# u and z token-major by seven products, with weight sums added onto kept pages

## The chip, the cores and the metric

The kernel runs on one core of a Trainium2 chip. The metric is the device time of one execution in microseconds; the kernel before has a median of 1637.15 us over three runs (1636.79 to 2001.78).

## The reference

Two layers over 512 tokens of width 2048, in float32. Both begin with a wide projection and end with an output projection, a residual sum and a layer norm. The part that matters here is the odd layer:

```python
def odd_layer(x, w_in, ln_g, ln_b, sgu_w, sgu_b, w_out):
    h = x @ w_in
    uv = jax.nn.gelu(h[..., :2 * D_SGU])
    z = h[..., 2 * D_SGU:]
    u, v = jnp.split(uv, 2, axis=-1)
    v = layer_norm(v, ln_g, ln_b).reshape(bsz, s // SGU_CHUNK, SGU_CHUNK, SGU_GROUPS, SGU_GROUP_DIM)
    w_causal = sgu_w * jnp.tril(jnp.ones((SGU_CHUNK, SGU_CHUNK), sgu_w.dtype))
    mixed = jnp.einsum('gts,bnsgc->bntgc', w_causal, v) + sgu_b.T[:, :, None]
    y = u * mixed.reshape(bsz, s, D_SGU) * jax.nn.silu(z)
    return y @ w_out
```

The even layer mixes a gated short convolution with an attention of three branches over eight heads; its output projection is `wo0`, the odd layer's projections are `wv1` (v), `wuz` (u and z) and `wo1`.

## The kernel before

Every float32 product is made of three products of rounded parts: `split` (lines 84 to 86) casts a page to a high part on ACT and subtracts it on DVE for the low part; then come high x high, high x low, low x high. Weights arrive as pages of 128x1024 (512 KB) from DRAM, asked for by SyncE into `raw` (four buffers); the parts `whi` and `wlo` have four buffers each.

The projections of the even layer go by `unit_a` (line 103): 128 weight columns stand still, 512 tokens move, 48 matmuls to a unit. Then come eight heads (the loop from line 436).

`wo0`, `wv1` and `wo1` go by `strassen` (line 528): the matrix is cut in two along the tokens, the contraction and the columns, and seven products p, in the order 1, 2, 5, 3, 6, 7, 4, take the place of eight. Each is 96 matmuls (lines 591 to 593), with pieces of x, `shi` and `slo`, standing still and a weight page moving. c is the half of a product's contraction, g the column group, m the token tile. Products 5, 7, 6 and 4 need sums of weight blocks. `weight_sums` (line 198) makes them ahead of time in DRAM with POOL's DMAs: a 1x1 copy that orders the step (208), a plain copy (210), an accumulating copy (212), all of 1024 KB blocks. The steps of `wo0` and `wv1` are issued two to a head, those of `wo1` in every second pass of the u/z loop.

u and z (line 817) go feature-major: for each of 16 column tiles j, one unit for u, one for z, then the mixing over positions as four 128x128 float32 matmuls (830) and DVE operations (832 to 835), with `row_sums` (797) once. v is normalised by one operation for each token tile (774). `residual_rows` (803) makes the scaled residual with rows `gb` and stores part of it for the last projection.

`drain` runs deferred work from the list `later`, so many pieces after each column group. The engines' instruction order comes from a scheduler, and POOL, SyncE, ACT and DVE each run theirs in order.

Around the start, `bias_rows` (178) takes two raw pages and line 317 a third, ahead of the next units.

Of the kernel before, what the change touches and what calls it, by code (L numbers as in the profile page):

```python
# [16 lines left out]
P = 128  # L17
# [48 lines left out]
def trunk(ctx, tc, xT, xn, oneh, cst, table, wa, wv, convw, posT, cw1, cw2, wo0, wuz, wv1, odg, odb, sguw, sgub, wo1, out):  # L66
# [102 lines left out]
    lnT = const.tile([P, 2 * KT], F32, name="lnT")  # L169
    convT = const.tile([P, 8, 3], F32, name="convT")  # L170
# [23 lines left out]
    def blk(w, k, n, g, c):  # L194

        return w[4 * (2 * g + n) + 2 * k + c]

    def weight_sums(w, name):

        t = {}  # L200

        def step(q, gcs):
            def run(after=None):

                for g, c in gcs:
                    t[q, g, c] = dram.tile([P, 2048], F32, name=f"{name}{q}{g}{c}")
                    if after is not None:
                        nc.gpsimd.dma_start(t[q, g, c][0:1, 0:1], after)
                    first = {5: lambda: blk(w, 0, 0, g, c), 7: lambda: blk(w, 1, 1, g, c), 6: lambda: t[7, g, c], 4: lambda: t[6, g, c]}[q]()
                    nc.gpsimd.dma_start(t[q, g, c], first)  # L210
# [3 lines left out]
        gcs = [(g, c) for c in range(2) for g in range(2)]  # L214
        return t, [step(q, gcs[i:i + 2]) for q in (5, 7, 6, 4) for i in (0, 2)]

    sums0, steps0 = weight_sums(wo0, "ts0_")
    sumsv, stepsv = weight_sums(wv1, "tsv_")
    sums1, steps1 = weight_sums(wo1, "ts1_")


    with ExitStack() as es:
# [218 lines left out]
        for h in range(NH):  # L441
# [23 lines left out]
            for st in (steps0 + stepsv)[2 * h:2 * h + 2]:  # L465
                st(qT[0:1, 0:1])
# [56 lines left out]
    def rows(ap):  # L523

        return ap if len(ap.shape) == 4 else ap.rearrange("p k (n c) -> p k n c", n=2)

    def strassen(sp, w, sums, a, done, given=None, more=2, by_tile=False, wx=None):
# [9 lines left out]
        def tt(out, x, y, op):  # L537
            nc.vector.tensor_tensor(rows(out), rows(x), rows(y), op)

        def s_piece(p, c, early):  # L540
            if p == 5 and c == 0:
                for d in range(2):
                    tt(a(1, 0, d), a(1, 0, d), a(1, 1, d), ALU.subtract)
            if p == 3 and c == 0:
                for d in range(2):
                    tt(a(0, 0, d), a(1, 0, d), a(0, 0, d), ALU.subtract)
                    tt(a(0, 1, d), a(0, 1, d), a(0, 0, d), ALU.add)
            if p == 6 and c == 0:
                for d in range(2):
                    o, x, y = a(1, 0, d), a(0, 0, d), a(1, 1, d)  # L550
                    for n in range(2) if len(o.shape) == 4 else (slice(None),):
                        nc.vector.scalar_tensor_tensor(o[:, :, n], x[:, :, n], -1.0, y[:, :, n], ALU.mult, ALU.subtract)
            if given and p in (1, 2, 4):
                return given(p, c)
            src = {1: a(0, 0, c), 2: a(0, 1, c), 5: a(1, 0, c), 3: a(0, 1, c), 7: a(1, 0, c), 6: a(0, 0, c), 4: a(1, 1, c)}[p]
            if early:
                hi = wp.tile([P, 4, 256], F32R, tag="hi", name="shi", bufs=4)
                lo = wp.tile([P, 4, 256], F32R, tag="lo", name="slo", bufs=4)
            else:
                hi = sp.tile([P, 4, 256], F32R, tag="shi", name="shi", bufs=2)  # L560
                lo = sp.tile([P, 4, 256], F32R, tag="slo", name="slo", bufs=2)
            split(rows(hi), rows(lo), rows(src))
            return hi, lo

        def unit(p, g, c):
            src = sums[p, g, c] if p in (5, 7, 6, 4) else blk(w, *{1: (0, 0), 2: (1, 0), 3: (1, 1)}[p], g, c)
            parts = []
            for d in range(2):
                raw = raw_page()
                nc.sync.dma_start(raw, src[:, d * 1024:(d + 1) * 1024])  # L570
                pool = wx if wx and count[0] % 2 else wp
                count[0] += 1
                hi = pool.tile([P, 1024], F32R, tag="hi", name="whi", bufs=4)
                lo = pool.tile([P, 1024], F32R, tag="lo", name="wlo", bufs=4)
                split(hi, lo, raw)
                parts.append((hi, lo))
            return parts

        banks = {}

        def product(p, g, c, m, s, parts):
            new = p in (1, 5, 7, 6)
            if new and c == 0:
                banks[g, m, p] = bank()
            b = banks[g, m, {2: 1, 3: 5, 4: 7}.get(p, p)]
            ms = slice(m * P, m * P + P)
# [105 lines left out]
    def normalized(m):  # L692
# [10 lines left out]
        def turn(c):  # L703
# [12 lines left out]
            split(act_hi[:, 4 * c:4 * c + 4, m * P:(m + 1) * P], act_lo[:, 4 * c:4 * c + 4, m * P:(m + 1) * P], dst)  # L716
# [12 lines left out]
    strassen(sp, wo0, sums0, quarters(y_sb), prefill)  # L729
# [35 lines left out]
    def given(p, c):  # L765
        t, k = {1: (0, 0), 2: (0, 1), 4: (1, 1)}[p]
        k0 = 8 * k + 4 * c
        return act_hi[:, k0:k0 + 4, t * 256:(t + 1) * 256], act_lo[:, k0:k0 + 4, t * 256:(t + 1) * 256]

    strassen(sp, wv1, sumsv, xq, done_v, given)  # L770
    drain(len(later))
    for m in range(NT):
        mv, rs = moments(statsv, m, EPS)
        nc.vector.tensor_scalar(xv[:, m], xv[:, m], mv[:, 0:1], rs, ALU.subtract, ALU.mult)
    sp_.close()


    yv = xv.rearrange("p n (j c) -> p j n c", c=P)
    xr = big.tile([P, NT, DM], F32, tag="big0", name="xr")
    with tc.tile_pool(name="sgu", bufs=2) as sg:  # L780
        swT = sg.tile([P, 8, P], F32, name="swT", bufs=1)
        nc.sync.dma_start(swT, sguw)
        tril = sg.tile([P, P], F32, name="tril", bufs=1)
        nc.sync.dma_start(tril, cst[:, P + NT:P + NT + P])
        nc.vector.tensor_tensor(swT, swT, tril[:, None, :].to_broadcast([P, 8, P]), ALU.mult)
        ones = sg.tile([P, P], F32, name="ones", bufs=1)
        nc.vector.memset(ones, 1.0)
        sbb = sg.tile([P, 8, P], F32, name="sbb", bufs=1)
        nc.sync.dma_start(sbb, sgub.to_broadcast([P, 8 * P]).rearrange("p (g t) -> p g t", g=8))
        ogT = sg.tile([P, 2, KT], F32, name="ogT", bufs=1)  # L790
        nc.sync.dma_start(ogT, odb)
        rw = sg.tile([P, 8, P], F32, name="rw", bufs=1)

        def row_sums():
            for c in range(2):
                ps = bank()
                nc.tensor.matmul(ps, ones, swT[:, 4 * c:4 * c + 4, :], start=True, stop=True)
                nc.vector.tensor_copy(rw[:, 4 * c:4 * c + 4, :], ps.rearrange("p (g t) -> p g t", g=4))

        def chunks(t):  # L800
            return t.rearrange("p (n t) -> p n t", n=NT)

        def residual_rows(g):

            cs = slice(g * 512, (g + 1) * 512)
            gb = sg.tile([P, 2, 512], F32, name="gb", bufs=1)
            for i in range(2):
# [159 lines left out]
```

## Time and profile before

| what | us |
|---|---|
| median of three runs | 1637.15 |
| the profiled execution | 1635.04 |
| its span, first to last instruction | 1633.0 |
| TensorE busy | 1603.1 |
| DVE busy | 859.1 |
| ACT busy | 589.6 |

The span holds the even layer with its heads (to about 772 us), `wo0` (to about 930), `wv1` (to 1110), u and z (to 1456), `wo1` (to about 1618) and the last rows. The profiled execution's time is 2.0 us longer than its span. Matmuls overlap in the records: the mean time of one is longer than the distance from one to the next.

### The profile page before, as it was taken

What the parts mean: (1) busy time and instruction counts of PE and PEld (TensorE: products, weight loads), DVE (VectorE), ACT (ScalarE), POOL (GpSimd) and SP (SyncE); (2) the same over time, 40 slices, a digit from 0 to 9 for tenths busy, and PEclk for the clock granted to TensorE, in tenths of its full rate; (3) what the DMA queues carried; (4) which work ended last, traced back from release to release, by engine and by line L of the source; (5) the groups of instructions that cost most, each with busy time, mean ns of one, the idle gap of its engine ahead of it and who ended that gap; (6) DMA issues with size and microseconds to landing.
All of it is one profiled execution on the core that took longest, in us unless ns stands there. A gap on an engine that the chain in (4) does not pass through costs nothing.

```text
span 1633.0 us, 19377 instructions
## 1 busy us (share of the span) xinstructions
PE 1603.1 (98%) x7527; PEld 1335.9 (82%) x7527; DVE 859.1 (53%) x1323; ACT 589.6 (36%) x859; POOL 150.7 (9%) x236
## 2 busy tenths in 40 slices
PE   8999999999999999999999999999999999998996
PEld 6798888888898888888888788888888888886884
DVE  5234444535325454445668985876433333355788
ACT  4123232323223232332555875542222222234641
POOL 0101020101001101010010000000111111100101
PEclk9999999999999999999999999999999999999998
DMA  6549595959249495866786665685777765669953
GB/s 218 196 152 271 135 250 132 267 158 247 76 154 243 149 243 156 217 184 179 217 243 205 239 217 193 199 306 181 220 198 200 195 189 167 182 181 293 274 190 135
DMA packets 98008, 328.56 MB, mean 201 GB/s; under 512 B 11443, under 2 KB 12243, under 8 KB 96380
## 3 DMA queue, kind: packets, MB, share of 16 engines
q1 hardware_dynamic: 65228, 217.30, 39.6%
q0 software_dynamic: 32544, 109.61, 28.8%
q8 instruction: 59, 0.97, 0.2%
q10 hardware_dynamic: 144, 0.41, 0.1%
q14 instruction: 33, 0.27, 0.1%
HBM read 315.72 MB, written 114.84 MB: 264 GB/s over the span
## 4 chain that ended last, share of the span: by engine, by line
PE 93%; issue 2%; DVE 2%; DMA 2%; ACT 0%; POOL 0%; SPq 0%; POOLq 0%; DVEq 0%
PE ps L111 19%; PE ps L113 19%; PE ps L112 19%; PE ps L593 8%; PE ps L592 8%; PE ps L591 8%; PE ps_t L397 1%; PE ps L122 1%; PE ps L120 1%; PE ps L121 1%; PE hp L286 1%; PE pm L830 1%; PE po L340 1%; PE po L342 1%; PE po L341 1%
## 5 line engine op out<-in xcount | busy, mean ns | idle before, releaser
L86 DVE TENSOR_TENSOR wlo<-raw,whi 128x1024 fp32r<-128x1024 f32 (+2 forms) x358 | 429.8, 1205 | 587.1 <-ACT whi L85 577.1
L85 ACT CAST whi<-raw 128x1024 fp32r<-128x1024 f32 (+2 forms) x358 | 371.1, 1038 | 908.8 <-PE ps L112 568.7
L111 PE MATMUL ps<-act_hi,whi 128*128 128x512 f32 x1376 | 542.4, 394 | 0.0
L113 PE MATMUL ps<-act_hi,wlo 128*128 128x512 f32 x1376 | 537.4, 391 | 1.3 <-DVE wlo L86 1.3
L112 PE MATMUL ps<-act_lo,whi 128*128 128x512 f32 x1376 | 535.4, 389 | 0.0
L113 PEld LDWEIGHTS ps<-act_hi,wlo 128*128 128x128 f32 x1376 | 258.3, 188 | 58.2 <-DVE wlo L86 1.7
L112 PEld LDWEIGHTS ps<-act_lo,whi 128*128 128x128 f32 x1376 | 258.5, 188 | 53.2
L111 PEld LDWEIGHTS ps<-act_hi,whi 128*128 128x128 f32 x1376 | 258.6, 188 | 51.1
L591 PE MATMUL ps<-whi,shi 128*128 128x512 f32 x576 | 224.6, 393 | 4.3 <-ACT ua L643 4.3
L593 PE MATMUL ps<-whi,slo 128*128 128x512 f32 x576 | 225.4, 392 | 0.6 <-DVE slo L86 0.5
L592 PE MATMUL ps<-wlo,shi 128*128 128x512 f32 x576 | 225.0, 391 | 0.2 <-DVE wlo L86 0.2
L591 PEld LDWEIGHTS ps<-whi,shi 128*128 128x128 f32 x576 | 108.1, 188 | 28.5 <-ACT ua L643 5.2
L593 PEld LDWEIGHTS ps<-whi,slo 128*128 128x128 f32 x576 | 108.2, 188 | 25.2 <-DVE slo L86 1.9
L592 PEld LDWEIGHTS ps<-wlo,shi 128*128 128x128 f32 x576 | 108.2, 188 | 24.9 <-DVE wlo L86 1.6
L212 POOL DMA_DIRECT2D ts<-in_wo_dram x32 | 33.2, 1038 | 161.5 <-DMA ts<-in_wo_dram 82.5
L378 ACT ACTIVATE t_sc<-t_sc,mx 128x128 f32<-128x128 f32 (+1 forms) x64 | 35.1, 550 | 17.2 <-DVE mx L375 17.2
L677 POOL TENSOR_TENSOR rs<-mv,epst 128x1 f32<-128x1 f32 x12 | 14.7, 1232 | 287.9 <-DVE mv L675 287.9
L591 PE MATMUL ps<-whi,act_hi 128*128 128x512 f32 x96 | 38.0, 399 | 0.6 <-ACT whi L85 0.6
L592 PE MATMUL ps<-wlo,act_hi 128*128 128x512 f32 x96 | 38.0, 396 | 0.0
L593 PE MATMUL ps<-whi,act_lo 128*128 128x512 f32 x96 | 37.9, 395 | 0.0
L122 PE MATMUL ps<-whi,act_lo 128*128 128x268 f32 x128 | 36.9, 288 | 0.0
L121 PE MATMUL ps<-wlo,act_hi 128*128 128x268 f32 x128 | 36.8, 288 | 0.0
(204 smaller groups left out, 1358.1 us busy)
## 6 DMA issues: line engine op xcount, KB each, us to landing
raw<-in_wa_dram SPq DMA_DIRECT2D x110, 512.0 KB, 5.3
ts<-in_wo_dram POOLq DMA_DIRECT2D x32, 1024.0 KB, 14.8
raw<-ts SPq DMA_DIRECT2D x64, 512.0 KB, 4.7
raw<-in_wuz_dram SPq DMA_DIRECT2D x64, 512.0 KB, 4.9
raw<-in_wo_dram SPq DMA_DIRECT2D x48, 512.0 KB, 5.2
tsv<-in_wv_dram POOLq DMA_DIRECT2D x16, 1024.0 KB, 12.9
raw<-tsv SPq DMA_DIRECT2D x32, 512.0 KB, 3.9
raw<-in_wv_dram SPq DMA_DIRECT2D x24, 512.0 KB, 3.9
```

The costliest lines, as they stand in the source:

```text
L85: nc.scalar.copy(hi, src)
L86: nc.vector.tensor_tensor(lo, src, hi.bitcast(F32), ALU.subtract)
L111: nc.tensor.matmul(ps, hi[:, w], act_hi[:, kt, :], start=kt == 0, stop=False)
L112: nc.tensor.matmul(ps, hi[:, w], act_lo[:, kt, :], start=False, stop=False)
L113: nc.tensor.matmul(ps, lo[:, w], act_hi[:, kt, :], start=False, stop=kt == KT - 1)
L121: nc.tensor.matmul(ps[:, :width], act_hi[:, kt, ms], lo[:, w], start=False, stop=False)
L122: nc.tensor.matmul(ps[:, :width], act_lo[:, kt, ms], hi[:, w], start=False, stop=kt == KT - 1)
L212: nc.gpsimd.dma_start(t[q, g, c], blk(w, *{5: (0, 1), 7: (0, 1), 6: (0, 0), 4: (1, 0)}[q], g, c), accum_op=ALU.add, max_dma_last_dim=2048)
L378: nc.scalar.activation(t[:, offs[qb]:offs[qb] + nk], t[:, offs[qb]:offs[qb] + nk], AF.Exp, bias=mx[:, qb:qb + 1], accum_out=sm[:, qb:qb + 1])
L591: nc.tensor.matmul(b, s[0][:, k, ms], hi[:, ws], start=new and c == 0 and k == 0, stop=False, **kw)
L592: nc.tensor.matmul(b, s[0][:, k, ms], lo[:, ws], start=False, stop=False, **kw)
L593: nc.tensor.matmul(b, s[1][:, k, ms], hi[:, ws], start=False, stop=c == 1 and k == 3, **kw)
```

## The change

- u and z are made in two runs r of `strassen`, each over half the columns of both. Their weight pages are four pieces of 256 columns (1 KB runs); the moving operand is then four pieces of 128 columns with a stride (`cuts`).
- The mixing is token-major: `swT` standing tiles and 256 columns a matmul; the bias is one number for each partition (`sbT`). v is normalised in pieces of 512 columns with rows (`values`), the residual rows likewise with tiles `xs` (two buffers) and `row` (one buffer).
- y is transposed on TensorE (`y_turn`) and copied by ACT, and goes to `wo1` from there. The rounded copies `act_hi` and `act_lo` of x in the odd layer go, `x_sums` keeps the sums of x apart in `exq`.
- `wuz` gets all four sums for both runs; `wo0`, `wv1`, `wo1` keep only the one for product 7 in DRAM. For 5, 6 and 4, `chained` loads a page x once (eight kept pages) and adds a block onto it by a POOL DMA before each of these products. The steps of sums, 20 of them, each of two blocks in 512 KB halves, are issued two or three to a head; the two steps of `wo1` at the head of u/z.
- Two more raw pages, two small transposes and a small store stand in the setup.
- The wide rows `gb` of the end are loaded after product 6 instead of 5. For the last product of `wo1`, only the second half goes tile by tile. The extra weight buffers there are two instead of four.

```diff
+    def uz_blocks(r):
+        def get(k, n, g, c, d):
+            q, e = 2 * r + g, (2 * k + c) * 512 + d * 256
+            return wuz[8 * q + n:8 * q + 8:2, :, e:e + 256].rearrange("i p e -> p i e")
...
-                    nc.gpsimd.dma_start(t[q, g, c], blk(w, *{5: (0, 1), 7: (0, 1), 6: (0, 0), 4: (1, 0)}[q], g, c), accum_op=ALU.add, max_dma_last_dim=2048)
+                    for d in range(2):
+                        src = get(*more[q], g, c, d)
+                        nc.gpsimd.dma_start(same(t[q, g, c, d], src), src, accum_op=ALU.add, max_dma_last_dim=1024)
...
+    sums0, steps0 = weight_sums(blocks(wo0), (7,), "ts0_")
+    early = steps0 + stepsv + stepsu[0] + stepsu[1]
...
+        bcol = raw_page()[:8, :P]
+        nc.sync.dma_start(bcol, sgub.rearrange("o (g t) -> (o g) t", g=8))
+        nc.tensor.transpose(ps[:, :8], bcol, ident[:8, :8])
+        ocol = raw_page()
+        nc.sync.dma_start(ocol[:, :2 * KT], odb.rearrange("p i k -> p (i k)"))
+        nc.tensor.transpose(ps[:2 * KT, :P], ocol[:, :2 * KT], ident)
...
-            for st in (steps0 + stepsv)[2 * h:2 * h + 2]:
+            for st in early[5 * h // 2:5 * (h + 1) // 2]:
...
+    def chained(get, sums, pool, direct):
+        def unit(p, g, c, d):
+            if p == 1 and c not in direct:
+                return page(g, c, d)
+            if p in (1, 2, 3):
+                if p == 2 and c in direct:
+                    page(g, c, d)
+                return raw_load(get(*{1: (0, 0), 2: (1, 0), 3: (1, 1)}[p], g, c, d))
+            if p == 7:
+                return raw_load(sums[p, g, c, d])
+            nc.gpsimd.dma_start(x[g, c, d], get(*{5: (0, 1), 6: (1, 1), 4: (1, 0)}[p], g, c, d), accum_op=ALU.add)
+            return x[g, c, d]
...
-        for j in range(KT):
-            ps = unit_a(wuz[2 * j])
-            ps = unit_a(wuz[2 * j + 1])
...
+        def one(m):
+            if m == 0:
+                gb[0] = row_pair(odrow, q)
+            v = xv[:, m, q * 512:(q + 1) * 512]
+            nc.vector.scalar_tensor_tensor(v, v, mom[m][0][:, 0:1], gb[0][:, 0], ALU.subtract, ALU.mult)
+            nc.vector.scalar_tensor_tensor(v, v, mom[m][1], gb[0][:, 1], ALU.mult, ALU.add)
...
+        def gate(t, g, m):
+            nc.vector.scalar_tensor_tensor(u[t, g, m], u[t, g, m], YSCALE, z[t, g, m], ALU.mult, ALU.mult)
+            for i in range(2):
+                nc.tensor.matmul(pm[:, i * 256:i * 256 + 256], swT[:, 2 * q + i, :], xv[:, mt, cs], start=True, stop=True)
+            for i in range(2):
+                nc.vector.scalar_tensor_tensor(xv[:, mt, cs], pm[:, i * 256:i * 256 + 256], sbT[:, 2 * q + i:2 * q + i + 1],
+                                               u[t, g, m][:, i * 256:i * 256 + 256], ALU.add, ALU.mult)
+            if r == 1:
+                later.append(lambda: y_turn(mt, q))
...
+        for r in range(2):
+            for q in (2 * r, 2 * r + 1):
+                values(q)
+            for q in (2 * r, 2 * r + 1):
+                residual_rows(q)
+            for st in steps1 if r == 0 else ():
+                st(swT[0:1, 0, 0:1])
+            strassen(sp, x_sums, plain(uz_blocks(r), sumsu[r]), uz_done(r), cuts=True)
...
-        strassen(sp, wo1, sums1, yq, take1, by_tile=True, wx=wx)
+        strassen(sp, in_place(yT), chained(blocks(wo1), sums1, fin, (0, 1)), take1, by_tile=True, wx=wx)
```

In the start, SyncE's loads stood like this before, where `in_odg` is the third raw page and `in_wa` a unit's weight pages:

```order
L184 DMA raw<-in_table_dram 32x8
L317 DMA raw<-in_odg_dram 32x128
L97 DMA raw<-in_wa_dram 128x1024 x2
L284 DMA raw<-in_cw_dram 128x1024 x2
L97 DMA raw<-in_wa_dram 128x1024 x2
```

And like this now, with `in_sgub` for bcol and `in_odb` for ocol:

```order
L186 DMA raw<-in_table_dram 32x8
L339 DMA raw<-in_odg_dram 32x128
L344 DMA raw<-in_sgub_dram 8x128
L349 DMA raw<-in_odb_dram 128x32
L97 DMA raw<-in_wa_dram 128x1024 x2
L306 DMA raw<-in_cw_dram 128x1024 x2
```

Two loads into raw pages moved in ahead of the unit's two weight pages.

At the head of u/z, DVE has in the first run's second half of product 1 and in product 2 (`xv` with `row` is v's normalising, `wlo` and `slo` the low parts of weights and of x):

```order
L86 TENSOR_TENSOR wlo<-raw,whi 128x1024
L873 SCALAR_TENSOR_TENSOR xv<-xv,mv,row 128x512 x2
L874 SCALAR_TENSOR_TENSOR xv<-xv,rs,row 128x512 x2
L86 TENSOR_TENSOR slo<-y_sb,shi 128x1024
L86 TENSOR_TENSOR wlo<-raw,whi 128x1024 x2
L873 SCALAR_TENSOR_TENSOR xv<-xv,mv,row 128x512 x2
L874 SCALAR_TENSOR_TENSOR xv<-xv,rs,row 128x512 x2
L86 TENSOR_TENSOR wlo<-raw,whi 128x1024 x2
```

Where one pass of j had four low parts and five other operations in 22.9 us, here four operations on v stand between each two low parts of the weights.

At the end of u/z TensorE went before from the last mixing straight into `wo1` (lines 591 to 593):

```order
L113 MATMUL ps<-act_hi,wlo 128x512
L830 MATMUL pm<-swT,xv 128x128 x4
L591 MATMUL ps<-whi,shi 128x512
L592 MATMUL ps<-wlo,shi 128x512
L593 MATMUL ps<-whi,slo 128x512
```

And now, where `pm` is the mixing, `ps_y` the transposes of y and lines 655 to 657 the products:

```order
L656 MATMUL ps<-wlo,shi 128x512
L657 MATMUL ps<-whi,slo 128x512
L897 MATMUL ps_y<-ident,xv 128x128 x8
L917 MATMUL pm<-xv,swT 128x256 x4
L897 MATMUL ps_y<-ident,xv 128x128 x6
L655 MATMUL ps<-whi,shi 128x512
L897 MATMUL ps_y<-ident,xv 128x128 x2
L656 MATMUL ps<-wlo,shi 128x512
```

The last two mixings and four groups of transposes stand in TensorE's order around `wo1`'s first matmul.

## Rows read from the trace of the kernel before

**Rows 1.** The page: the span, and each engine's busy time.

```profile
span 1633.0 us, 19377 instructions
...
PE 1603.1 (98%) x7527; PEld 1335.9 (82%) x7527; DVE 859.1 (53%) x1323; ACT 589.6 (36%) x859; POOL 150.7 (9%) x236
```

**Rows 2.** Busy time by stretch: us, five engines, granted clock, DMA share, GB/s.

```profile
880.00:930.00 50.00, 50.00 (x238) 41.38 (x237) 48.85 (x77) 35.81 (x49) 2.44 (x3) 1.00 0.64 221
...
1110.00:1456.00 346.00, 346.00 (x1574) 285.66 (x1573) 135.41 (x164) 79.02 (x92) 29.27 (x42) 1.00 0.66 187
...
1480.00:1500.00 20.00, 15.71 (x68) 12.15 (x66) 10.85 (x9) 9.03 (x11) 0.00 (x0) 1.00 1.07 305
```

**Rows 3.** TensorE's waits: for what, us in total, times, the longest.

```profile
PE ps L591 <- ACT ua L643: 4.3, 2, 2.5
```

**Rows 4.** ACT's timeline before 1491 us: start, length, line, what; idle before it.

```profile
1489.77 1.04 ACT L85 CAST whi<-raw 128x1024 fp32r<-128x1024 f32 x1 [1.75 <-DMA raw<-in_wo_dram]
1490.72 0.58 ACT L643 COPY ua<-ps 128x512 f32<-128x512 f32 x1
```

**Rows 5.** The chain of waits, TensorE's transposes, row sums and mixing: start, length.

```profile
903.33 0.87 PE ps_x L708 x8
...
1110.08 1.72 PE ps L797 x4
...
1157.57 0.89 PE pm L830 x8
...
1180.45 0.89 PE pm L830 x8
```

**Rows 6.** Groups of instructions by form: busy us, mean ns; idle before.

```profile
L86 DVE TENSOR_TENSOR wlo<-raw,whi 128x1024 fp32r<-128x1024 f32 x342 | 416.2, 1222 | 542.2 <-ACT whi L85 532.2 <-PE pm L830 4.3 <-PE ps_t L397 4.2
...
L830 PE MATMUL pm<-swT,xv 128*128 128x128 f32 x128 | 16.9, 275 | 0.0
...
L286 PE MATMUL hp<-tokb,raw 128*128 128x62 f32 x128 | 14.9, 288 | 0.0
...
L833 DVE SCALAR_TENSOR_TENSOR ug<-ug,th 128x512 f32<-128x512 f32 x16 | 11.1, 691 | 0.4
```

**Rows 7.** TensorE's timeline after the bias rows.

```profile
56.15 0.24 PE L319 MATMUL ps<-ident,raw 32*128 32x32 f32 x1
56.32 0.50 PE L111 MATMUL ps<-act_hi,whi 128*128 128x512 f32 x1
```

**Rows 8.** SyncE's timeline there: when the next page is asked for.

```profile
56.25 0.35 SPq L97 DMA_DIRECT2D raw<-in_wa_dram  x1
```

**Rows 9.** DMA issues: count, KB each, median us from issue to landing.

```profile
ts<-in_wo_dram POOLq DMA_DIRECT2D x32, 1024.0 KB, 14.8
...
raw<-in_wuz_dram SPq DMA_DIRECT2D x64, 512.0 KB, 4.9
...
xr<-xhat SPq DMA_DIRECT2D x16, 256.0 KB, 6.1
...
xres<-xr SPq DMA_DIRECT2D x12, 256.0 KB, 2.3
...
gb<-in_odg_dram SPq DMA_DIRECT2D x8, 256.0 KB, 5.2
```

**Rows 10.** The page's DMA queues: packets, MB, share of 16 engines' span.

```profile
q1 hardware_dynamic: 65228, 217.30, 39.6%
q0 software_dynamic: 32544, 109.61, 28.8%
```

**Rows 11.** Busy time by stretch in one head; columns as in rows 2.

```profile
127.00:180.00 53.00, 52.33 (x261) 44.45 (x260) 25.61 (x71) 16.81 (x39) 9.18 (x17) 1.00 0.96 260
180.00:203.00 23.00, 23.00 (x111) 19.32 (x110) 8.50 (x11) 6.12 (x9) 0.00 (x0) 1.00 0.27 90
```

**Rows 12.** Busy time by stretch, two early stretches; columns as in rows 2.

```profile
8.00:20.00 12.00, 9.74 (x34) 7.29 (x33) 8.71 (x8) 8.45 (x9) 0.00 (x0) 0.86 1.02 401
...
52.00:60.00 8.00, 6.72 (x27) 4.60 (x27) 3.30 (x6) 0.00 (x0) 0.74 (x1) 1.00 0.27 85
```

More of the change, by code (lines that the diff above doesn't have):

```diff
@@ L200, in weight_sums, with same, run @@
+    def same(t, src):
+        return t.rearrange("p (i e) -> p i e", i=4) if len(src.shape) == 3 else t
+    GCS = [(g, c) for c in range(2) for g in range(2)]
+    def weight_sums(get, qs, name):
         t = {}
+        first = {5: (0, 0), 7: (1, 1)}
+        more = {5: (0, 1), 7: (0, 1), 6: (0, 0), 4: (1, 0)}
         def step(q, gcs):
-            def run(after=None):
+            def run(after):
                 for g, c in gcs:
[L206 to L210, printed above, removed]
+                    for d in range(2):
+                        h = t[q, g, c, d] = dram.tile([P, 1024], F32, name=f"{name}{q}{g}{c}{d}")
+                        nc.gpsimd.dma_start(h[0:1, 0:1], after)
+                        src = get(*first[q], g, c, d) if q in first else t[{6: 7, 4: 6}[q], g, c, d]
+                        nc.gpsimd.dma_start(same(h, src), src)
@@ L211, in run @@
                 for g, c in gcs:
-                    nc.gpsimd.dma_start(t[q, g, c], blk(w, *{5: (0, 1), 7: (0, 1), 6: (0, 0), 4: (1, 0)}[q], g, c), accum_op=ALU.add, max_dma_last_dim=2048)
-            return run
[L214 to L219, printed above, removed]
+                    for d in range(2):
+                        src = get(*more[q], g, c, d)
+                        nc.gpsimd.dma_start(same(t[q, g, c, d], src), src, accum_op=ALU.add, max_dma_last_dim=1024)
@@ L222, in trunk @@
+            return run
+        return t, [step(q, GCS[i:i + 2]) for q in qs for i in (0, 2)]
+    sums0, steps0 = weight_sums(blocks(wo0), (7,), "ts0_")
+    sumsv, stepsv = weight_sums(blocks(wv1), (7,), "tsv_")
+    sums1, steps1 = weight_sums(blocks(wo1), (7,), "ts1_")
+    sumsu, stepsu = zip(*(weight_sums(uz_blocks(r), (5, 7, 6, 4), f"tu{r}_") for r in range(2)))
+    early = steps0 + stepsv + stepsu[0] + stepsu[1]
     with ExitStack() as es:
@@ L549, in s_piece @@
                 for d in range(2):
[L550 to L562, printed above, removed]
+                    nc.vector.scalar_tensor_tensor(a(1, 0, d), a(0, 0, d), -1.0, a(1, 1, d), ALU.mult, ALU.subtract)
@@ L563, in s_piece, with strassen, weights @@
+    def strassen(sp, src, unit, done, more=2, by_tile=False, wx=None, cuts=False):
+        count = [0]
+        def s_piece(p, c):
+            hi = sp.tile([P, 4, 256], F32R, tag="shi", name="shi", bufs=2)
+            lo = sp.tile([P, 4, 256], F32R, tag="slo", name="slo", bufs=2)
+            split(hi, lo, src(p, c))
             return hi, lo
-        def unit(p, g, c):
-            src = sums[p, g, c] if p in (5, 7, 6, 4) else blk(w, *{1: (0, 0), 2: (1, 0), 3: (1, 1)}[p], g, c)
+        def weights(p, g, c):
@@ L575, in unit @@
+                lo = pool.tile([P, 1024], F32R, tag="lo", name="wlo", bufs=2 if pool is wx else 4)
                 split(hi, lo, raw)
@@ L790, in trunk @@
[L790 to L801, printed above, removed]
```

247 lines of the change are left out of this document (156 added, 91 removed).

## The prediction

> **What bounds the kernel now.** I read the page's busy times first, then the busy time by stage, then the chain of waits. TensorE is busy for 1603.1 us of a span of 1633.0 [rows 1], so the time is, to within 30 us, the number of matmuls times their pitch, and every other engine counts only where TensorE waits for it. By stage TensorE is full, 346.00 of 346 us in the u/z stage; the one hole of note after the start is 1480 to 1500 us, at the head of the last projection, where it is busy for 15.71 of 20 us while the DMA engines stand at their limit (share 1.07) [rows 2]. There it waits 4.3 us in two gaps that the list of waits puts down to an ACT copy [rows 3]; but that copy stands behind a cast that waited 1.75 us for a weight page from DRAM [rows 4], so the pages are what is late.
>
> The pitch comes from the chain. In u/z the four mixing matmuls of one j return every 22.88 us (1157.57 to 1180.45) and take 0.89 us; between them lie two units of 48 matmuls, so one matmul with 512 moving columns costs (22.88 - 0.89)/96 = 0.229 us [rows 5]. The profiled run took 1635.04 us, 2.1 less than the median of 1637.15: I sum against the run and add 2.1 at the end.
>
> **Matmuls: what goes and what comes.** The 32 units of u and z have 32 x 48 = 1536 matmuls. Two runs of seven products, each 7 x 2 x 2 x 2 x 4 x 3 = 672, make 1344. So 192 go: -192 x 0.229 = -44.0 us. The row sums (L797) go: -1.7 [rows 5]. The mixing was 16 x 0.89 = 14.2 us. After it is 32 matmuls with 256 fp32 columns; four with 128 columns take 0.89, so 0.22 each, and 62 columns cost the same as 128 (288 against 275 ns a record) [rows 5, 6]. If weight loading sets the price they cost 7.1 us, if columns do, 32 x 0.445 = 14.2. I take 14.2: no change. The y transposes are new: 64 of 128x128; eight records take 0.87, so 64 x 0.109 = +7.0 [rows 5]; two small ones at the start, +0.3. Sum on TensorE: -38.4 us.
>
> A gap that goes: the 4.3 us of [rows 3]. The pages were late there beside the last sums of wo1 and the wide rows gb (two of 1024 KB); in the change wo1's sums are begun at the head of u/z and are one of four, and gb is asked for two products later. -4.3.
>
> **What becomes late: the start.** After the bias-row matmuls TensorE goes on at 56.32 us with a page that is already split [rows 7]; SyncE issues the next page at 56.25 [rows 8]. In the change two more raw pages (bcol, ocol) are taken and loaded ahead of it, of a pool of four, and TensorE's order has two small transposes in front of the unit. ocol gets its page only when the bias rows' page is free, at about 56 us, the transpose waits for its load, and the unit's first page for the page behind that. A page takes about 5 us to land [rows 9] and 1.05 to cast [rows 4], so TensorE comes back near 62 instead of 56.3. +5 (2 to 7).
>
> **The head of u/z.** Before, DVE was busy for 135 of 346 us in u/z [rows 2] and never in TensorE's way. In the change it has, in each product and column group (24 matmuls, 24 x 0.229 = 5.5 us of TensorE), two low parts at 1.22, half a low part of x, 0.6, and about four 512-wide operations at about 0.7: 5.9 us [rows 6]. It is in order, and those operations wait for rows: a row pair of 256 KB lands 5.2 us after its issue, into a tile with one buffer, so that the next pair starts only when the last reader is done; the residual's piece takes 6.1 us to come and 2.3 to go, with two buffers [rows 9]. Behind a waiting DVE stand the low parts; behind a waiting SyncE (its stores wait for DVE) stand the weight pages. Four pages of lookahead are two groups, 11 us. It lasts for some sixteen groups. If the scheduler's order holds, only the DVE surplus of 0.4 x 16 and little else is seen: 2 to 6; if each of the four row pairs costs a half landing, about 12 more. I take +9 (2 to 17).
>
> **Middle and end of u/z.** Products 6 and 7 carry four or five operations a group more (adds, silu, gate): +4 for both runs (0 to 8). At the end TensorE's order has the last mixing matmuls and sixteen transposes between or ahead of wo1's first matmuls, and the last two gates hang on DVE: after the last product it does one add, two multiplies, two pairs of 256-wide operations (0.4 each, a little over half of 0.69), and two low parts that stand between, 3 x 0.69 + 4 x 0.4 + 2 x 1.22 = 6.1 us [rows 6], with a gelu (as an ACT copy of 512 columns, 0.6 [rows 4]) and one mixing (0.9) in the chain: 7.6 us. TensorE's own work there is 16 x 0.109 + 2 x 0.89 = 3.5 us, of which the 0.9 lies in that chain. +5 (2 to 8).
>
> **Projections.** The kept page takes an accumulate by POOL's queue in place of a load of a finished sum. q1, the plain queue, used 39.6% of the span for 217.30 MB: 1633 x 0.396/217.3 = 2.98 us a MB. q0 used 28.8% for 109.61 MB: 4.29 [rows 10]. About half of q0's bytes are plain copies; at 2.98 for them the accumulates come to 5.8 us a MB. So a 0.524 MB page costs 1.56 loaded, 2.25 to 3.06 accumulated. wo1: 40 loads, 62 us; 24 accumulates, 54 to 73; 12 residual adds of 0.26 MB at 4.29, 14; the final rows, 6: 136 to 155 us, against 672 x 0.229 = 154 of TensorE. wo0 is 6 us less, with what is left of the even layer's sums ahead of it. It fits, barely, with a whole product of lookahead (eight kept pages). wo0 with its entry +4 (0 to 17), wv1 +1, wo1 +3 (0 to 17).
>
> The Trainium skill's page "DMA: Bandwidth & Descriptors", section "Bandwidth", advises batches of 1 MiB or more; the change cuts its sums from 1024 KB to 512. By the fit in its section "Anatomy of one DMA", 2.0 us and the bytes at 436 GB/s, two halves take 6.4 us where the whole takes 4.4, an estimate. Here such a fixed part shows as landing time (14.8 us for 1024 KB, 4.9 for a 512 KB page [rows 9]); with the queue full it need not add to the engines' time, so the sum above has none of it.
>
> **Even layer.** A head lasts about 76 us (127 to 203); its DMA comes to 53 x 0.96 + 23 x 0.27 = 57 us [rows 11]. Its two steps were 4.2 MB copied and 4.2 accumulated, 12.5 + 24.3 = 37, so 20 are other work. After, 2.5 steps on average: 5.24 MB each way, 15.6 + 30.4, with 20: 66 of 76 us. No loss, if an accumulate in runs of 1 KB costs per byte what one in runs of 2 KB did, which no row shows.
>
> **Sum.** -38.4 - 4.3 + 5 + 9 + 4 + 5 + 4 + 1 + 3 = -11.7. The tail after wo1 is the same work in nearly the same order, 0. 1635.04 - 11.7 = 1623.3, plus 2.1: **1625 us**, 0.7% less.
>
> **Rivals.** A measurement of this kernel tells about 2% from no change: faster is below 1604, slower above 1670.
>
> *The stalls stay hidden.* For it: TensorE kept 50.00 of 50 us in the busiest stretch of wo0, 880 to 930, with DVE at 48.85 [rows 2]. Against it: no rows had to land there. With 2 at the start, 2 at the head, 2 at the end: 1635 - 42.7 + 6 + 2.1 = 1600.
>
> *Slower: accumulates in short runs fill the DMA queue in the even layer.* POOL issues in order, so sums that run late hold back the bc copies of a head to come, then wo0's first accumulates. It decides where a MB costs over (76 - 20 - 15.6)/5.24 = 7.7 us, 1.3 times 5.8. If a run of 1 KB costs as much as one of 2 KB it is 11.6: 97 us a head against 76, about +160 over eight heads; half way, 8 us a head or 65. From the forecast: 1690 to 1785. For it: step phases already stand at share 0.96; against it: the two queues' prices per MB are near two to one, as if bytes read set them.
>
> *The projections are at the queue's end.* With 3.06 a page and the landing chain in series, +14 each in wo0 and wo1 beyond what I have: 1650.
>
> *The moving operand in four pieces of 128 columns costs more.* L286's strided columns give no sign of it [rows 6]; at double price +308 us.
>
> *The clock falls in the gaps.* At the start the granted clock was 0.86, at 52 to 60, with TensorE busy for 6.72 of 8 us, 1.00 [rows 12]. The gaps I add are a few times longer. A restart like the first costs 0.14 x 12 = 1.7 us; four of them +7: 1632. The Trainium skill's "TensorE: Matmul & The Clock Gate", Part 1, has the throttled clock as the default, which activity releases; the 0.86 of the start in [rows 12] agrees.
>
> **Chances.** Forecast 0.47; hidden 0.25; full queue 0.10; projections 0.12; pieces 0.02; clock 0.04. Faster by over 2%: the hidden case and a little of the forecast, 0.27; slower: full queue and pieces, 0.12; within 2%: 0.61. The range goes from the hidden case with cheap mixing (7 us less), 1594, to just past the projections at their limit, 1660.
>
> **What would show it.** TensorE's matmuls down by 192 x 0.229; a gap at 56 to 62 us; DVE low parts late at the head of u/z, with DVE's waits on row or xs and SyncE's stores before weight pages; a gap before wo1's first matmul that ends with DVE L920. The forecast is wrong if u/z's pitch is not 0.229, if the heads grow beyond 76 us, or if TensorE's holes sum to less than 15 us or over 60.

## The result, and the profile after

The changed kernel took 1683.97 us (median of four runs, 1680.29 to 1684.66) beside 1637.83 for the kernel before: a ratio of 1.0279, 95% interval 1.0259 to 1.0300. The forecast was 1625, 0.7% faster, with a range of 1594 to 1660. One execution of before's, of 2001.78 us, was disturbed and is left out of the ratio.

The page after, with the lines that answer to [rows 1] and [rows 10]:

```profile
span 1682.3 us, 19662 instructions
...
PE 1590.3 (95%) x7333; PEld 1318.9 (78%) x7333; DVE 967.5 (58%) x1438; ACT 686.2 (41%) x965; POOL 317.4 (19%) x429
...
q0 software_dynamic: 72896, 139.00, 41.1%
q1 hardware_dynamic: 84684, 216.78, 38.5%
```

TensorE is busy for 12.8 us less than before in a span that is 49.3 us longer: it waits. (Its busy time holds matmuls at a lower clock too, so it fell by less than its work.) DVE and ACT have some 100 us more work each, POOL's queue moves 29 MB more and takes 41.1% of the engines' time in place of 28.8%.

Busy time by stretch, as in [rows 2]; the columns are the stretch, its length, the busy time of TensorE, its weight loads, DVE, ACT and POOL, then the granted clock, the DMA share and GB/s:

```profile
500.00:540.00 40.00, 40.00 (x195) 33.67 (x194) 21.65 (x56) 14.86 (x35) 12.49 (x19) 1.00 1.01 228
800.00:840.00 40.00, 30.01 (x118) 22.71 (x116) 13.95 (x12) 16.33 (x19) 7.16 (x9) 0.94 1.08 278
840.00:880.00 40.00, 32.12 (x125) 25.97 (x126) 22.18 (x21) 14.57 (x16) 11.16 (x13) 0.84 0.98 195
1120.00:1160.00 40.00, 25.91 (x101) 20.19 (x99) 24.65 (x34) 13.29 (x17) 14.81 (x21) 0.87 1.03 254
1400.00:1440.00 40.00, 40.00 (x178) 33.15 (x177) 28.45 (x35) 22.37 (x25) 0.00 (x0) 1.00 0.53 174
1520.00:1560.00 40.00, 34.43 (x138) 26.85 (x138) 16.39 (x15) 17.88 (x21) 9.65 (x12) 0.95 1.06 284
```

One reads down the DMA share: in `wo0`, at the head of u/z and in `wo1` it stands near 1.0, TensorE has holes (30.01 of 40, 25.91 of 40), and the granted clock is below 1 as well. A full queue does not make a hole by itself: in the heads, at 500, the share is 1.01 and TensorE is busy for 40.00 of 40. In the second run of u/z, at 1400, the share is 0.53, TensorE is full and its 178 matmuls in 40 us show the old pitch. 

What TensorE waits for, by the list that [rows 3] is taken from (us in total, times, the longest):

```profile
PE ps L656 <- DVE wlo L86: 37.3, 17, 9.8
PE ps L655 <- ACT whi L85: 20.8, 7, 6.7
...
PE ps L111 <- ACT whi L85: 3.8, 1, 3.8
...
PE ps L351 <- DMA raw<-in_odb_dram: 1.6, 1, 1.6
```

Most of it is waiting for parts of weight pages. To see what makes them late, one place is followed through three engines, the head of u/z. SyncE asks for a row pair and for pages:

```profile
1130.03 2.26 SPq L862 DMA_DIRECT2D row<-odrow  x2
1132.39 16.55 SPq L577 DMA_DIRECT2D raw<-in_wuz_dram  x4
```

DVE, which needs the rows for v, and ACT, which needs the pages:

```profile
1131.06 2.35 DVE L86 TENSOR_TENSOR wlo<-raw,whi 128x1024 fp32r<-128x1024 f32 x2
1143.31 1.41 DVE L873 SCALAR_TENSOR_TENSOR xv<-xv,mv,row 128x512 f32<-128x512 f32 x2 [9.90 <-DMA row<-odrow]
...
1146.18 2.35 DVE L86 TENSOR_TENSOR wlo<-raw,whi 128x1024 fp32r<-128x1024 f32 x2
```
```profile
1136.23 1.04 ACT L85 CAST whi<-raw 128x1024 fp32r<-128x1024 f32 x1 [9.24 <-DMA raw<-in_wuz_dram]
```

The row pair, asked for at 1130, has landed at 1143: thirteen us where [rows 9] had 5.2. The page that ACT casts at 1136 was asked for at 1126.2, ten us before, and ACT idles for 9.24. DVE stands for 9.90 with the low parts of 1146 queued behind the rows. So both branches of my step "head of u/z" are there, but with longer landings than the 5 to 6 us that I took. From 1110 to 1220 (count, KB each, median us from issue to landing):

```profile
raw<-in_wuz_dram SPq DMA_DIRECT2D x18, 512.0 KB, 9.9
...
row<-in_odg_dram SPq DMA_DIRECT2D x4, 256.0 KB, 10.8
```

The row pairs of `odrow`, of which the one at 1130 is the slowest, have 6.2 in the median.

In these 110 us POOL's queue moves 8.39 MB of `wo1`'s sums. The kernel before moved 8.39 MB of them in the same 110 us too, with TensorE busy for 110.00 of 110; but the plain queue had 14.04 MB there in place of 19.97, so the share was 0.71 in place of 0.95. It is the two together that fill the engines.

TensorE's first matmuls behind such a gap (start, length):

```profile
1159.86 0.80 PE L655 MATMUL ps<-whi,shi 128*128 128x512 f32 x1 [6.67 <-ACT whi L85]
1160.45 0.63 PE L656 MATMUL ps<-wlo,shi 128*128 128x512 f32 x1
1160.88 0.63 PE L657 MATMUL ps<-whi,slo 128*128 128x512 f32 x1
```

And the stretch's row:

```profile
1159.80:1163.00 3.20, 3.14 (x7) 2.49 (x8) 0.98 (x2) 2.38 (x4) 1.67 (x4) 0.50 1.02 249
```

They come 0.43 us apart, not 0.229: after 6.67 us of waiting the granted clock is 0.50, its lower level (1.2 of 2.4 GHz).

From such starts I made a ledger: for each 20 us, the distance from one matmul to the next, less 0.229 (a shorter instruction: its length); stretches of over 1.2 us summed by stage. It holds gaps and slow matmuls both.

| stage | before | after | forecast, added |
|---|---|---|---|
| first load, to 20 us | 6.3 | 6.5 | 0 |
| setup, 40 to 80 us | 1.5 | 7.6 | 5 |
| wo0, 772 to 960 | 0 | 24.9 | 4 |
| head of u/z, 1110 to 1220 | 0 | 35.1 | 9 |
| rest of u/z's first run | 0 | 5.8 | 4 |
| wv1 | 0 | 0 | 1 |
| end of u/z and wo1 | 6.3 | 22.6 | 5 + 3 - 4.3 |
| sum | 14.1 | 102.5 | 26.7 |

The last matmul starts at 1667.17 after and 1617.88 before, +49.3; with 88.4 more lost, TensorE's own work is 39.1 us less. The forecast had 38.4. The ledger is an estimate: how short instructions are counted moves its sums by 2 to 3 us. Counting only matmuls 0.33 to 0.48 us apart, the lower clock's share of the loss is 24.0 us after and 3.2 before.

### The profile page after: what moved, and what is told of

It is laid out like the page before. It is cut to its first block, busy times and chain, and to the rows that moved or that the text cites. A ratio compares the mean times of both kernels' runs of the same rounds, so it can differ in the third digit from the quotient of the medians.

```text
span 1682.3 us, 19662 instructions
## 1 busy us (share of the span) xinstructions
PE 1590.3 (95%) x7333; PEld 1318.9 (78%) x7333; DVE 967.5 (58%) x1438; ACT 686.2 (41%) x965; POOL 317.4 (19%) x429
## 3 DMA queue, kind: packets, MB, share of 16 engines
q0 software_dynamic: 72896, 139.00, 41.1%
q1 hardware_dynamic: 84684, 216.78, 38.5%
## 4 chain that ended last, share of the span: by engine, by line
PE 78%; DMA 12%; DVE 5%; issue 3%; ACT 1%; POOL 1%; SPq 0%; DVEq 0%; POOLq 0%; ACTq 0%
PE ps L111 12%; PE ps L113 12%; PE ps L112 12%; PE ps L656 11%; PE ps L657 10%; PE ps L655 10%; DMA x<-in_wo_dram 4%; DVE wlo L86 2%; DMA row<-odrow 2%; DMA row<-in_odg_dram 1%; PE ps_t L430 1%; DMA xv<-xres 1%; PE ps L122 1%; DMA xres<-xs 1%; PE ps L121 1%
## 5 line engine op out<-in xcount | busy, mean ns | idle before, releaser
L656 PE MATMUL ps<-wlo,shi 128*128 128x512 f32 x1120 | 447.7, 400 | 37.6 <-DVE wlo L86 37.3
L655 PE MATMUL ps<-whi,shi 128*128 128x512 f32 x1120 | 447.4, 402 | 21.4 <-ACT whi L85 20.8
L657 PE MATMUL ps<-whi,slo 128*128 128x512 f32 x1120 | 443.9, 397 | 1.3 <-DVE slo L86 1.3
L111 PE MATMUL ps<-act_hi,whi 128*128 128x512 f32 x864 | 340.6, 394 | 3.8 <-ACT whi L85 3.8
L113 PE MATMUL ps<-act_hi,wlo 128*128 128x512 f32 x864 | 337.7, 391 | 0.0
L112 PE MATMUL ps<-act_lo,whi 128*128 128x512 f32 x864 | 337.5, 391 | 0.0
L656 PEld LDWEIGHTS ps<-wlo,shi 128*128 128x128 f32 x1120 | 215.5, 192 | 92.0 <-DVE wlo L86 46.9
L655 PEld LDWEIGHTS ps<-whi,shi 128*128 128x128 f32 x1120 | 215.1, 192 | 70.4 <-ACT whi L85 23.7
L657 PEld LDWEIGHTS ps<-whi,slo 128*128 128x128 f32 x1120 | 215.2, 192 | 47.5 <-DVE slo L86 2.0
L111 PEld LDWEIGHTS ps<-act_hi,whi 128*128 128x128 f32 x864 | 162.9, 189 | 36.5 <-ACT whi L85 4.0
L86 DVE TENSOR_TENSOR wlo<-x,whi 128x1024 fp32r<-128x1024 f32 x80 | 96.9, 1220 | 44.1 <-ACT whi L85 43.5
L227 POOL DMA_DIRECT2D tu<-qT x64 | 39.7, 843 | 102.1 <-ACT qT L486 101.4
L411 ACT ACTIVATE t_sc<-t_sc,mx 128x128 f32<-128x128 f32 (+1 forms) x64 | 35.1, 550 | 17.3 <-DVE mx L408 17.3
```

What stands on the lines that cost most here:

```text
L86: nc.vector.tensor_tensor(lo, src, hi.bitcast(F32), ALU.subtract)
L111: nc.tensor.matmul(ps, hi[:, w], act_hi[:, kt, :], start=kt == 0, stop=False)
L112: nc.tensor.matmul(ps, hi[:, w], act_lo[:, kt, :], start=False, stop=False)
L113: nc.tensor.matmul(ps, lo[:, w], act_hi[:, kt, :], start=False, stop=kt == KT - 1)
L227: nc.gpsimd.dma_start(h[0:1, 0:1], after)
L411: nc.scalar.activation(t[:, offs[qb]:offs[qb] + nk], t[:, offs[qb]:offs[qb] + nk], AF.Exp, bias=mx[:, qb:qb + 1], accum_out=sm[:, qb:qb + 1])
```

## The experiments

Three causes stood to choose from. A: the DMA engines are full at wo0's start, the head of u/z and wo1, so every landing is late. B: the single row buffer and the two xs buffers make DVE and SyncE wait in turn, whatever the load. C: the accumulating DMA onto a kept page is itself too dear. A and C do not exclude each other, since dear adds also fill the engines.

**e1_ts1_later.** wo1's sums are called in u/z's second run.

```diff
-            for st in steps1 if r == 0 else ():
+            for st in steps1 if r == 1 else ():
```

> The two steps of wo1's sums (8 MB copied and added in DRAM, DMA share 1.0 from 1120 to 1200 us) move from the head of u/z to the start of its second run, where the DMA share was 0.53 to 0.62. Theory A (the DMA engines are full there, so rows and pages land late): TensorE's lost time between 1110 and 1220, 32 us with the slow clock, falls to under 12, and the time falls by 15 to 25 us. Rival B (one buffer for the rows and two for xs make DVE and SyncE wait in turn, whatever the DMA load): the loss stays over 25 us and the time within 6 us.

Measured 1684.76, ratio to before 1.0292 (1.0274 to 1.0309). It tells nothing, for the steps did not move. POOL's timeline of e1, where L227 is the small copy ahead of a step:

```profile
1117.95 2.69 POOL L227 DMA_DIRECT2D ts<-swT  x5 [29.91 <-issue]
```

Here the scheduler puts an instruction where its inputs are ready, and the position in the program matters little. Only a data dependency holds it back; e5 uses one.

**e2_row2.** Row pairs with two buffers.

```diff
-            gb = sg.tile([P, 2, 512], F32, tag="row", name="row", bufs=1)
+            gb = sg.tile([P, 2, 512], F32, tag="row", name="row", bufs=2)
```

> The row pairs get two buffers instead of one; nothing else changes. Rival B: the waits of DVE on row DMAs at the head of u/z (9.9 and 6.1 us) go, and the time falls by 10 to 20 us. Theory A: the rows are asked for earlier but the queue is as full, so other landings become late in their place: 0 to 7 us less.

1685.57, ratio 1.0291 (1.0272 to 1.0311): nothing gained. DVE's waits for residual pieces and rows, first after, then in e2 (us in total, times, longest):

```profile
DVE xs L887 <- DMA xs<-xhat: 18.1, 7, 6.0
...
DVE xv L873 <- DMA row<-odrow: 14.1, 3, 9.9
```
```profile
DVE xs L887 <- DMA xs<-xhat: 28.5, 7, 8.5
...
DVE xv L873 <- DMA row<-odrow: 3.3, 1, 3.3
```

The wait for v's rows fell from 14.1 us to 3.3, and the wait for xs went from 18.1 to 28.5. The wait only changed its place, as A says. This is a test of the row buffer alone; the two xs buffers of B were not varied.

**e3_sums_later.** Four steps of wuz's sums leave the heads.

```diff
-    early = steps0 + stepsv + stepsu[0] + stepsu[1]
+    early = steps0 + stepsv + stepsu[0] + stepsu[1][:4]
...
-            for st in early[5 * h // 2:5 * (h + 1) // 2]:
+            for st in early[2 * h:2 * h + 2]:
...
-            for st in steps1 if r == 0 else ():
+            for st in steps1 if r == 0 else stepsu[1][4:]:
```

> The last four steps of the second run's sums of wuz leave the heads (then two steps to a head, sixteen in all) and are issued at the start of the second run of u/z. Theory A for wo0 (sums left over from the last heads fill the DMA engines when wo0 starts): the loss of 26 us between 772 and 960 falls to under 8, and the time falls by 15 to 25 us, less what the sums cost in the second run. Rival C (the accumulating DMAs onto kept pages are by themselves too dear or too late in the chain): the loss stays over 18 us.

1708.57, ratio 1.0436 (1.0420 to 1.0451). As in e1 the scheduler hoisted them, to the head of u/z. This makes it a test from both sides; two stretches of e3:

```profile
840.00:880.00 40.00, 39.12 (x166) 32.22 (x167) 23.76 (x21) 21.29 (x24) 12.03 (x14) 0.96 0.96 223
1160.00:1200.00 40.00, 23.99 (x68) 16.92 (x67) 13.68 (x16) 10.24 (x12) 12.60 (x19) 0.74 1.08 273
```

By the ledger wo0 loses 10.8 us in place of 24.9, and u/z from 1100 to 1300 loses 78.4 in place of 40.9. The same sums cost where they meet a full queue. The 10.8 is neither of the values on record, under 8 for A and over 18 for C: the leftover sums are a part of wo0's loss and not all of it.

**e4_no_add.** The kept pages are overwritten, not added to.

```diff
-            nc.gpsimd.dma_start(x[g, c, d], get(*{5: (0, 1), 6: (1, 1), 4: (1, 0)}[p], g, c, d), accum_op=ALU.add)
+            nc.gpsimd.dma_start(x[g, c, d], get(*{5: (0, 1), 6: (1, 1), 4: (1, 0)}[p], g, c, d))
```

> The 72 DMAs onto the kept pages copy instead of adding, so the products 5, 6 and 4 of wo0, wv1 and wo1 take wrong sums; queue, order and waits are the same. Rival C: an added page costs about twice a copied one, so wo0 and wo1 (share 1.0 there) lose 10 to 20 us less each, the time falls by 25 us or more. Theory A (leftover sums in wo0, late rows elsewhere): the loss in wo0 falls by under 10 us, in wo1 by under 8; the time by 5 to 15.

1656.67, ratio 1.0122 (1.0105 to 1.0140): 27 us less than the change. The ledger: wo0 12.5 for 24.9, the end of u/z and wo1 10.4 for 22.6, the head of u/z 35.5, as in the change. By the values on record this is C (25 us or more in all, 10 to 20 each in wo0 and wo1). Its queue:

```profile
span 1658.6 us, 19662 instructions
...
q0 software_dynamic: 72896, 139.00, 36.2%
```

0.362 x 1658.6 = 600 us against 0.411 x 1682.3 = 691: 91 us for the 72 pages, 37.75 MB, or 2.41 us a MB above the 2.98 of a plain copy. So, as an estimate that takes e4's copies at the plain queue's price, an added page costs 2.83 us and a loaded one 1.56. The price lies inside my bounds (2.25 to 3.06); C holds in that adding is dear, and A in that half of wo0's loss and all of u/z's are not from it.

**e5_ts1_run1.** wo1's sums wait for a tile of the second run.

```diff
-            for st in steps1 if r == 0 else ():
-                st(swT[0:1, 0, 0:1])
...
                     nc.scalar.copy(ua[g, m], b)
+                    if r == 1 and (g, m) == (1, 1):
+                        for st in steps1:
+                            st(ua[g, m][0:1, 0:1])
```

> In e1 the steps had stayed at the head of u/z, since they waited for nothing that came later; here they wait for a copy of the second run's first product, so that the 8 MB really move to about 1360 us. Theory A (full DMA engines at the head of u/z): the loss between 1110 and 1220 falls from 34 us to under 15, the second run (share 0.55) takes the sums at under 5 us, and the time falls by 13 to 25 us. Rival B (waits in turn on rows and xs): the loss stays over 25 us, the time within 6.

1659.05, ratio 1.0134 (1.0115 to 1.0154): 25 us less.

```profile
1120.00:1160.00 40.00, 37.27 (x161) 29.49 (x160) 33.89 (x45) 19.04 (x22) 2.31 (x2) 1.00 0.74 214
1160.00:1200.00 40.00, 36.53 (x153) 29.38 (x152) 28.12 (x31) 21.87 (x25) 0.00 (x0) 0.96 0.86 285
1340.00:1400.00 60.00, 60.00 (x282) 50.02 (x281) 32.26 (x28) 33.87 (x42) 7.46 (x9) 1.00 1.07 295
```

The head of u/z has shares of 0.74 and 0.86 and loses 9.2 us in the ledger, not 35.1. With both buffers as they were, that is A and not B. And at 1340 to 1400, with the sums running and a share of 1.07, TensorE is busy for 60.00 of 60. The landing of u/z's pages in e5, first from 1110 to 1220, then from 1340 to 1400:

```profile
raw<-in_wuz_dram SPq DMA_DIRECT2D x20, 512.0 KB, 5.3
```
```profile
raw<-in_wuz_dram SPq DMA_DIRECT2D x8, 512.0 KB, 10.3
```

At the head the pages land after 5.3 us in place of 9.9. At 1340 they land as late as they did at the head in the change, and nothing is lost: neither a full queue nor late pages are by themselves a loss. This stretch reads hardly anything but pages, which are asked for four ahead, while the head of u/z reads rows and residual pieces that DVE waits for in order. That this is the difference is argued from the two orders; no run tests it by itself.

**e6_setup_moved.** The two small loads, transposes and the store go to the second head (`if h == 1`), the lines unchanged but for the store's queue.

```diff
-        nc.gpsimd.dma_start(odrow.rearrange("i (k p) -> (i k) p", p=P), ocol[:2 * KT, P:2 * P])
+                nc.sync.dma_start(odrow.rearrange("i (k p) -> (i k) p", p=P), ocol[:2 * KT, P:2 * P])
```

> The two small loads into raw pages, their transposes and the store go from the setup to the second head. The start's part of the loss (5.4 us of gaps at 56 to 62 and the slow matmuls behind them, less the 1.3 us gap of before) goes: 4 to 7 us less. If the gap is only moved to the late pages behind it: 0 to 2.

1676.72, ratio 1.0242 (1.0219 to 1.0264): 7.3 us less than the change: all of the setup's 6.1 in the ledger, as near as the runs' spread of 7 us can tell.

**e7_long_runs.** Product 7's sums of wo0, wv1 and wo1 in longer runs.

```diff
-                        nc.gpsimd.dma_start(same(t[q, g, c, d], src), src, accum_op=ALU.add, max_dma_last_dim=1024)
+                        nc.gpsimd.dma_start(same(t[q, g, c, d], src), src, accum_op=ALU.add, max_dma_last_dim=4096)
```

> The sums of product 7 for wo0, wv1 and wo1 (six of the 22 steps) add in runs of 4 KB instead of 1 KB; those of wuz keep 1 KB, which their layout sets. If short runs are what makes adding dear (by the queues' totals 7.0 us a MB at 1 KB, 5.84 at 2 KB, 5.4 at 4 KB), 12.6 MB get 1.6 us a MB cheaper, 20 us of DMA time, a third of it at the head of u/z: 4 to 10 us less. If not: within 3 us.

1685.38, ratio 1.0295 (1.0277 to 1.0314): no change. A miss in the time (4 to 10 us less were expected), though the DMA work did fall:

```profile
span 1683.7 us, 19662 instructions
...
q0 software_dynamic: 63680, 139.00, 40.1%
```

0.401 x 1683.7 = 675 us, 16 less for 12.6 MB: 1.3 us a MB. But two thirds of these adds run in the heads, where TensorE is full anyway, and the others left the losses at the head of u/z as they were.

**e8_spread.** e5 and e6 (their lines are left out here), and two steps of sums in the setup, so that the last head has one step.

```diff
+    for st in early[:2]:
+        st(pos[0:1, 0, 0:1])
+    cut = [2, 4, 7, 9, 12, 14, 17, 19, 20]
...
-            for st in early[5 * h // 2:5 * (h + 1) // 2]:
+            for st in early[cut[h]:cut[h + 1]]:
```

> e5 and e6 together, and two steps of sums are issued in the setup (DMA share 0.08 from 30 to 52 us), so that the last head has one step instead of three. Theory A: the gains of e5 and e6, and in wo0 10 to 15 us more, as in e3: 1640 to 1655 in all. Rival C (the added pages themselves): wo0 keeps over 18 us, 1655 to 1665.

1658.70, ratio 1.0133 (1.0117 to 1.0150): missed. wo0 did gain (12.0 for 24.9), but a new hole opened:

```profile
60.00:127.00 67.00, 51.86 (x315) 46.93 (x314) 12.85 (x14) 11.41 (x16) 9.91 (x20) 0.85 0.77 223
800.00:840.00 40.00, 37.85 (x165) 30.48 (x164) 23.14 (x20) 20.83 (x25) 9.12 (x11) 1.00 1.02 283
```

In POOL's order the store of the bias rows stood behind the two steps, and TensorE is busy for 51.86 of 67 us, with one wait of 14.9 us for a page.

**e9_spread2.** As e8, with the two steps behind the first heads' bias copies.

```diff
         cmp_out(0)
+        for st in early[:2]:
+            st(k_f[0][0:1, NC2:NC2 + 1])
```

> As e8, but the two early steps stand behind the bias rows and the first heads' bias copies in POOL's order, so that nothing of the setup waits for them. The loss of e8 between 60 and 80 us (14.8) goes, the rest stays: with theory A 1638 to 1648. If the early steps only move the load into the first heads: 1650 or more.

1641.62 (eight runs), ratio 1.0025 (1.0014 to 1.0035): as theory A had it.

**e10_kept.** As e9, with fewer loads in wo1.

```diff
-        strassen(sp, in_place(yT), chained(blocks(wo1), sums1, fin, (0, 1)), take1, by_tile=True, wx=wx)
+        strassen(sp, in_place(yT), chained(blocks(wo1), sums1, fin, (0,)), take1, by_tile=True, wx=wx)
```

> As e9, and in wo1 product 1 takes its second half's pages from the kept pages, as wo0 does: four 512 KB loads less where the DMA share is 1.0. With theory A wo1's loss of some 18 us falls by 4 to 8 against e9; if the kept pages' room comes free too late, wo1 starts later instead: 0 to 6 us more than e9.

1635.83 (ten runs), ratio 0.9994 (0.9984 to 1.0004): 5.8 us less than e9, for four pages (4 to 8 expected).

**e11_kept_all** and **e12_kept_both.** The same with all of wo1's product 1 from kept pages; e12 in wo0 also.

```diff
-        strassen(sp, in_place(yT), chained(blocks(wo1), sums1, fin, (0, 1)), take1, by_tile=True, wx=wx)
+        strassen(sp, in_place(yT), chained(blocks(wo1), sums1, fin, ()), take1, by_tile=True, wx=wx)
...
-    strassen(sp, in_place(quarters(y_sb)), chained(blocks(wo0), sums0, xc, (0,)), prefill)
+    strassen(sp, in_place(quarters(y_sb)), chained(blocks(wo0), sums0, xc, ()), prefill)
```

> As e10, and in wo1 product 1 takes all its pages from the kept ones: four 512 KB loads less again, 6 us of DMA time at share 1.0. Theory A: 2 to 6 us less than e10 (1630 to 1634). If the kept pages' room comes free only after u/z's last gates, wo1's first matmuls wait: 2 to 8 us more than e10.

> As e11, and the same in wo0: four loads less where the DMA share is 0.95 to 1.0 from 772 to 880. Theory A: 3 to 8 us less than e11. If the kept pages' room there comes free only when the even layer's buffers do, wo0 starts late: 2 to 10 us more than e11.

e11: 1634.89, ratio 0.9973 (0.9959 to 0.9988). e12: 1635.46, ratio 0.9997 (0.9986 to 1.0009). Both missed what was expected, 2 to 6 and 3 to 8 us less: e10, e11 and e12 lie within 1 us of each other, and the runs of e11 alone spread over 9. e11 has the lowest median, 49 us below the change; beside before it is 0.3% by the ratio and 0.1% by the medians (1636.79), so it is a draw with a kernel that needs none of this. e12's ledger has new losses of about 5 us before 800. The largest of TensorE's waits in e11, where line 660 is one of the products:

```profile
PE ps L660 <- DVE wlo L86: 18.8, 13, 3.2
```

## Why the prediction was wrong

**TensorE's own sum held.** -38.4 forecast, -39.1 by the ledger. Matmul count, the pitch of 0.229 (also with the moving operand in four pieces), row sums, transposes and mixing need no correction as a sum. Of the mixing's two prices the one by columns, which I took, is the nearer: its 64 records with 256 columns start 0.215 us apart in the median, those with 128 columns 0.112 before. The other terms were not taken apart.

**The start held**: +5 forecast, 6.1 in the ledger, 7.3 by e6. The wait is where it was put: TensorE's L351 on ocol's load and L111 on the page behind it.

**"The head of u/z", +9, is the step that failed most**: 35.1. I priced rows and residual pieces at the landing times of [rows 9], 5 to 6 us, though 8 MB of sums stand at this very place, on POOL's queue, beside 6 MB of plain loads that the kernel before did not have there. I counted the two steps when I took a gap away from wo1 ("begun at the head of u/z") and left them out where they arrive. e5 shows it: without them the pages land after 5.3 us in place of 9.9, and the stage loses 9.2. That is near the 9, but the 9 was the middle of 2 to 17, and whether its parts are the ones that I added up no run shows; the match may be luck. The sign that I had set for a wrong forecast, holes of over 60 us in sum, came: 88.4 more than before.

**"wo0 with its entry", +4, range to 17**: 24.9. I had the leftover sums of the last heads in words and not in the sum; in e3, e8 and e9, without them, wo0 loses 10.8, 12.0 and 12.8, so they are about half. With the leftovers still there but no adds, e4 also loses only 12.5. So each of the two loads costs about half, and the halves add up to the whole. At the longest stop DVE stands in front of a residual. Its timeline after, where L697 takes statistics of a token tile onto which POOL adds the residual:

```profile
843.39 0.69 DVE L697 BATCH_NORM_STATS2 stats<-xv 128x6 f32<-128x512 f32 x1 [13.06 <-issue]
844.00 1.21 DVE L86 TENSOR_TENSOR wlo<-x,whi 128x1024 fp32r<-128x1024 f32 x1
...
853.54 0.69 DVE L697 BATCH_NORM_STATS2 stats<-xv 128x6 f32<-128x512 f32 x1 [5.46 <-DMA xv<-in_xn_dram]
```

TensorE's longest wait, 9.80 us, ends behind the low parts that follow the first of these. For that one the profile names no releaser, but the residual's add that POOL issued at 827.59 landed at 843.22, 0.2 us before the operation began; it took 15.6 us:

```profile
xv<-in_xn_dram POOLq DMA_DIRECT2D x1, 256.0 KB, 15.6
```

The next of its kind waits for such an add by name. A kernel with that operation later in DVE's order was not tried.

**wo1**, +3 and a gap of 4.3 taken away: with the end of u/z, 22.6 in place of 6.3. The budget of 136 to 155 us of DMA beside 154 of TensorE "fits, barely" was right as a sum and wrong as a forecast: 2.83 a page is near my upper end, and a sum that just fits leaves nothing for a landing that comes late. e4 (10.4 us lost) and e10 (5.8 us less for four loads) show the DMA load to be the cause; which wait turns it into lost time was not tested.

**The rivals.** "The projections are at the queue's end" was the right mechanism for two of the three places, priced at 1650. "Accumulates in short runs" did not decide: of the queue's 691 us what is neither (55 MB, nearly all copies, at 2.98) takes 164 and the added pages (37.75 MB at 5.4) 204, which leaves for 46.1 MB added in runs of 1 KB about 7.0 us a MB, an estimate, under the 7.7 from which it would have. The even layer ends in time (708.98 of 712 us busy from 60 to 772), though its last sums run over into wo0, as this rival had them do. Its prices were summed wrongly: half way, at 8.7 us a MB, a head has 81 us of DMA for its 76, so some 40 us over eight heads and not 65. The short runs of the plain loads are no rival either: the plain queue has 84684 packets in place of 65228, and a MB costs 0.385 x 1682.3 / 216.78 = 2.99 us, before 2.98. "The clock falls in the gaps" was given +7; it is 21 us of the loss, since there are twelve gaps of over 2 us (two before), not four. So the lower clock adds about a third to what the waits themselves cost.

## What to carry to other kernels

Price a DMA at the share that the queue will have when it runs, with everything that is there already: at the head of u/z the share went from 0.71 to 0.95, and pages landed after 9.9 us in the median (6.3 in the kernel before) and one row pair after thirteen. Where a stretch must have full queues, choose one that reads little but pages asked for well ahead: the heads at 500 and e5 at 1340 lost nothing at shares of 1.01 and 1.07. A step that is to run later needs a data dependency; its place in the program alone did not move it here (e1, e3).

## What the runs showed of the hardware

Adding by DMA cost 5.4 us a MB of the engines' time in 4 KB runs onto kept pages against 2.98 copied, and about 7.0 in 1 KB runs in DRAM; e7, where 12.6 MB went from 1 KB to 4 KB, saved 1.3 of these. All of it is worked out from e4, e7 and the queues' totals. TensorE's matmuls behind a gap of 6.67 us ran 0.43 us apart at a granted clock of 0.50, and from 1163 to 1166 the clock was back at 0.97; behind the 2.54 us of the kernel before, at 1491 us, the first came 0.34 apart and the next 0.23, and the clock of 1488 to 1496 was 1.00. The Trainium skill's "TensorE: Matmul & The Clock Gate", Part 1, has idle time bring the throttled clock back and activity release it. The first place agrees; at the second no fall is seen.
